# Output projection of a hybrid diffusion layer: seven half-size products in place of eight, with the norm, the stores and the neighbouring sums laid out anew

## The chip, the cores and the metric

The kernel runs on one core of a Trainium2 chip. The metric is the device time of one execution in microseconds (us), the median of several runs. The engines are TensorE (PE; its weight loads are listed as PEld), VectorE (DVE), ScalarE (ACT), GpSimd (POOL) and SyncE (SP), which issues the DMAs. Each works through its own list of instructions in order and waits on semaphores of the others.

## What is computed

One layer over 1024 latent tokens of width 1024. Its part that matters here, with `merged` the gated sum of an attention and a retention branch:

```python
y  = (merged) @ w_out                 # 1024 x 1024 by 1024 x 1024
x1 = x + gate1 * y                    # gated residual
n  = x1 * rsqrt(mean(x1 * x1, -1) + 1e-6)
h2 = n * (g2 * (1 + scale2)) + shift2 # modulated, feeds the gated MLP
u  = h2 @ w_up ; conv ; silu-gate ; @ w_down
out = final_norm(x1 + gate2 * mlp)
```

## The kernel before

**Numbers.** Every fp32 operand is split into a high part and a remainder (`split`, L85: a cast on ScalarE, L86, and a subtraction on VectorE, L87). A product is three matmuls: high by high, high by low, low by high (`mm3`, `open3` at L1372).

**Seven products.** Several matrix products are done by the Strassen-Winograd scheme: both operands are cut into 2 by 2 quarters, sums S1 to S4 of one and T1 to T4 of the other are formed, and seven products of quarters take the place of eight (`Seven`, L1376). That holds before the change for the merge gates, the up projection (from its third unit on; a unit is the product for one pair of column blocks) and the down projection, but not for the output projection.

**Stages around the change**, in the order of the text, which is nearly the order on each engine:

- *Gates* (748 to 924 us): the products of the merge gates. Beside them POOL makes sums of quarters of `w_down` (`down_sums`, L1238, subtraction at L1249): SP loads four tiles `pj` of 128 x 512, POOL makes four subtractions, SP stores the four results to `d_w`, from which the down projection loads them later. Blocks 0 to 4 are made beside retention, blocks 5 to 8 here (at every third step, L1540), blocks 9 and 10 in the next stage.
- *Merge* (924 to 1007 us): for each of 8 channel blocks `db` and both token halves `pret` (L1588) multiplies retention by its projection, VectorE multiplies by the gate, POOL adds the attention part (L1593), and the result is split into `mh`, `ml`. SP loads `w_out`, split into `wo` (L1620 to L1636).
- *Output projection* (1007 to 1100 us): `out_proj` (L1638) goes over 8 blocks of 128 tokens and two column halves, 24 matmuls into a bank `om` each (L121 to L123). VectorE multiplies by `gate1` (L1650) and adds the rows of `x` (L1651); SP stores the rows `x1`; ScalarE squares them and sums (L1654), VectorE and POOL turn that into the norm's factor (L1655, L1656), VectorE scales (L1657, `xn`). `norm_out` (L1660) of the block before transposes `xn` on PE, and ScalarE and VectorE modulate it into `h2` (L1677 to L1680); in the second half VectorE makes the token sums T1 to T4 of each block (L1686 to L1689) and SP stores them to `d_t`.
- *Up projection* (from about 1100 us): two plain units (L1838) whose products need no sums, with the depthwise convolution `conv` (L1754) after each; `comb` (L1780) loads and splits the token sums T1 and T2 in the first, T3 and T4 in the second. Then come the units in seven products, interleaved. The first product with a T operand is the second one of unit 2. Their weight sums are made on POOL (L1383 to L1386).
- *Down projection* (L1858 on): seven products of 11 steps, with the sums of products, the gated residual on POOL (L1946, L1947), the squares on ScalarE (L1897) and the final norm.

Of the kernel before, what the change touches and what calls it, by code (L numbers as in the profile page):

```python
# [16 lines left out]
P = 128  # L17
# [23 lines left out]
def tile_hybrid_layer(ctx, tc: tile.TileContext, io, dbg=None):  # L41
# [18 lines left out]
    d_h = dram.tile([NTB // 2, P, KB, P], F32, name="d_h")  # L60
    d_t = dram.tile([4, NTB // 2, P, KB // 2, P], F32, name="d_t")
# [1176 lines left out]
    def down_sums(pool_, j0, j1, bufs=8):  # L1238
        def load(j, n):
            t = pool_.tile([P, 512], F32, tag="pj", bufs=bufs, name="pj")  # L1240
            sync.dma_start(t, io["w_down"][n % 2, NH * (n // 2) + j])
            return t

        ts, store = [load(j0, n) for n in range(4)], None
        yield
        for j in range(j0, j1):
            nxt = []
            for n, (c, x, y, o) in enumerate(((1, 1, 0, 0), (3, 3, 1, 1), (2, 3, 0, 3), (4, 2, 3, 2))):
                late(pool.tensor_tensor(ts[o], ts[x], ts[y], ALU.subtract))  # L1249
                if store:  # L1250
                    sync.dma_start(*store)
                store = (d_w[j, c - 1], ts[o])
                if j + 1 < j1:
                    nxt.append(load(j + 1, n))
# [121 lines left out]
    class Seven:  # L1376
# [24 lines left out]
        def step(self, n):  # L1401
# [7 lines left out]
            elif n == 1:  # L1409
                self.prod(self.Y, self.s2, "T2", True, False)  # L1410
# [150 lines left out]
    gpool = [sb(f"gates{i}", "right") for i in range(2)]  # L1561

    def gtile(half, dt, name):
        return gpool[half].tile([P, 512], dt, tag="g", bufs=2 * KB + 1, name=name)

    sg = {}

    def merge_load(db, halves=(0, 1)):
        for half in halves:
            sg[db, 0, half] = gtile(half, F32, "sg")  # L1570
            sync.dma_start(sg[db, 0, half], d_pn[db, half])
            sg[db, 1, half] = t = gtile(half, F32, "sg")
# [11 lines left out]
    pjp = sb("out_sums", "right")  # L1584
    out_sums = down_sums(pjp, GATE_SUMS, NH, 7)
    mg = {}

    def pret(db, half):  # L1588
        m = g_ps("pr")
        mm_a(m, wp[db], lambda k: orr[half, k][0], lambda k: orr[half, k][1])  # L1590
        g = sg[db, 1, half]
        vec.tensor_tensor(g, m, g, ALU.mult)
        (vec if db == KB - 1 else pool).tensor_tensor(g, g, sg[db, 0, half], ALU.add)  # L1593
        h_, l_ = gtile(half, F32R, "mh"), gtile(half, F32R, "ml")
        split(h_, l_, g)
        mg[db, half] = (h_, l_)


    merge_load(0, (0,))
# [3 lines left out]
    wp[1] = pret_load(1)  # L1603
    merge_load(1, (0,))
    for half in range(2):
        if half:
            merge_load(0, (1,))
            merge_load(1, (1,))
        for db in range(2):
            pret(db, half)  # L1610
    for db in range(2, KB):
        wp[db] = pret_load(db)
        merge_load(db)
        if db == 2:
            brow(0, gate1)
        for half in range(2):
            pret(db, half)
            next(out_sums, None)
    pjp.release()
    wo = {}  # L1620
    for kb in range(KB):
        t = wop.tile([P, 2, 512], F32R, tag="wo", bufs=KB, name="wo")
        wo[kb, 0] = wload(io["w_out"][0, kb], into=t)
# [5 lines left out]
    h2p = sb("h2", "left")  # L1629
    h2 = [[h2p.tile([P, 2, 512], F32R, tag="h2", bufs=KB, name="h2a") for _ in range(KB)], None]  # L1630
    op = sb("outp", "right")
    po = ps("out_ps", "left")
    pu = [ps("u_ps0", "right")]
    for kb in (6, 7, 0, 1, 2, 3, 4, 5):
        t = (wop if kb >= 6 else op).tile([P, 2, 512], F32R, tag="wx", bufs=2, name="wx") if kb >= 4 else None
        wo[kb, 1] = wload(io["w_out"][1, kb], into=t)  # L1636

    def out_proj(tb):  # L1638
        half, ts = tb // 4, slice((tb % 4) * P, (tb % 4 + 1) * P)
        x1 = op.tile([P, D], F32, tag="x1", bufs=3, name="x1")  # L1640
        xr = op.tile([P, D], F32, tag="xn", bufs=2, name="xn")
        sync.dma_start(x1, io["x"][tb * P : (tb + 1) * P])
        for dh in range(2):
            cs = slice(dh * 512, dh * 512 + 512)
            m = po.tile([P, 512], F32, tag="o", bufs=2, name="om")
            for kb in range(KB):
                wc = wo[kb, dh]
                h_, l_ = mg[kb, half]
                mm3(m, h_[:, ts], l_[:, ts], wc[:, 0], wc[:, 1], kb == 0, kb == KB - 1)
            vec.tensor_tensor(xr[:, cs], m, gate1[:, cs], ALU.mult)  # L1650
            vec.tensor_tensor(x1[:, cs], xr[:, cs], x1[:, cs], ALU.add)  # L1651
        sync.dma_start(d_x1[tb * P : (tb + 1) * P], x1)
        ss = op.tile([P, 2], F32, tag="ss", bufs=2, name="ss")
        act.activation(xr, x1, AF.Square, accum_out=ss[:, 0:1])  # L1654
        vec.tensor_scalar(ss[:, 0:1], ss[:, 0:1], 1.0 / D, EPS, ALU.mult, ALU.add)  # L1655
        pool.tensor_tensor(ss[:, 1:2], ss[:, 0:1], mhalf[:, 0:1], ALU.pow)  # L1656
        vec.tensor_scalar(xr, x1, ss[:, 1:2], None, ALU.mult)  # L1657
        return xr

    def norm_out(tb, xr):  # L1660
        half, ts = tb // 4, slice((tb % 4) * P, (tb % 4 + 1) * P)
        if tb == 4:
            h2[1] = [(gtile(0, F32R, "h2h"), gtile(0, F32R, "h2l")) for _ in range(KB)]
        vr = op.tile([P, KB, P], F32, tag="v", bufs=2, name="v")
        if half:
            vo = op.tile([P, KB, P], F32, tag="vo", bufs=1, name="vo")
            sync.dma_start(vo, d_h[tb - 4])
        for kg in range(2):
            tp = po.tile([P, 4, P], F32, tag="t", bufs=2, name="tp2")
            for k in range(4):  # L1670
                pe.transpose(tp[:, k], xr[:, (kg * 4 + k) * P : (kg * 4 + k + 1) * P], ident)
            for k in range(4):
                kb = kg * 4 + k
                t = h2[half][kb]
                h_, l_ = (t[:, 0, ts], t[:, 1, ts]) if half == 0 else (t[0][:, ts], t[1][:, ts])
                a, sh = a2[:, kb : kb + 1], col[:, 24 + kb : 25 + kb]
                act.activation(h_, tp[:, k], AF.Identity, bias=sh, scale=a)  # L1677
                v = vr[:, kb]
                vec.tensor_scalar(v, tp[:, k], a, sh, ALU.mult, ALU.add)  # L1679
                vec.tensor_tensor(l_, v, h_.bitcast(F32), ALU.subtract)  # L1680
        if half == 0:
            sync.dma_start(d_h[tb], vr)
            return

        (b11, b21), (b12, b22) = [(t[:, : KB // 2], t[:, KB // 2 :]) for t in (vo, vr)]
        vec.tensor_tensor(b11, b12, b11, ALU.subtract)  # L1686
        vec.tensor_tensor(b12, b22, b12, ALU.subtract)
        vec.tensor_tensor(b22, b22, b11, ALU.subtract)
        vec.tensor_tensor(b21, b21, b22, ALU.subtract)  # L1689
        for c, t in enumerate((b11, b22, b12, b21)):  # L1690
            sync.dma_start(d_t[c, tb - 4], t)

    xr = None
    for tb in range(NTB):
        nx = out_proj(tb)
        if tb:
            norm_out(tb - 1, xr)
        xr = nx


    def up(u, wu, half):
        h = h2[half]
        hi, lo = ([t[:, i] for t in h] if half == 0 else [t[i] for t in h] for i in range(2))
        mm_a(u[:, half * 512 : half * 512 + 512], wu, lambda k: hi[k], lambda k: lo[k])

    def up_load(j, br):
        return [wload(io["w_up"][j, br, i]) for i in range(2)]

    def u_tile(n):
        return pu[n // 2 % 2].tile([P, T], F32, tag="u", bufs=2, name="u")  # L1710

    early = []
    for br in range(2):
        early.append((u_tile(br), up_load(0, br)))
        up(*early[br], 0)
    norm_out(NTB - 1, xr)
    po.release()
    pu.append(ps("u_ps1", "left"))
# [12 lines left out]
    A11, A12, A22, S1, S2, S3, S4 = range(7)  # L1731

# [47 lines left out]
    def comb(c):  # L1780
        t = [tpl.tile([P, 4, KH, P], F32R, name=f"T{c}{i}") for i in range(2)]
        for b in range(4):
            raw = ur_load(d_t[c, b])
            split(t[0][:, b], t[1][:, b], raw.rearrange("p (k t) -> p k t", k=KH))
# [4 lines left out]
    class Up(Seven):  # L1789
# [11 lines left out]

        def banks(self):
            t = u_tile(2 * self.n)
            self.X, self.Y = t[:, 0:512], t[:, 512:1024]
            self.Z = u_tile(2 * self.n + 1)[:, 0:512]
            self.u = [tap.tile([P, T], F32, tag="uu", bufs=4, name="uu") for _ in range(2)]

        def moving(self, c):
            if c[0] == "T":
                h_, l_ = combs[c]  # L1810
                return [(h_[:, :, k], l_[:, :, k]) for k in range(KH)]
# [3 lines left out]
        def dst(self, b, half):  # L1815
            return self.u[b][:, half * 512 : half * 512 + 512]
# [4 lines left out]
        def done(self, b, half):  # L1821
            if (b, half) == (0, 1):
                conv(self.j, *self.u)

# [262 lines left out]
```

## Time and profile before

| | |
|---|---|
| time, median of 3 runs | 1764.97 us (1764.35 to 1765.2) |
| profiled execution, first to last instruction (span) | 1759.2 us |
| between this span and the median of the runs | 5.8 us |
| TensorE busy | 1726.0 us, 98% |
| VectorE busy | 1284.2 us, 73% |
| ScalarE busy | 849.2 us, 48% |
| GpSimd busy | 539.3 us, 31% |
| mean granted TensorE clock | 0.996 |

The durations come from one profiled execution; the times from separate runs. The profiled execution's own time is known only as its span. The profile names each group of instructions by its line, engine and tiles (output <- inputs); `idle before` is the time that the engine waited ahead of it, with the releaser. Matmuls are pipelined: one lasts 0.39 us in the records, while the next starts earlier, so their rate is read from starts.

### The profile page before, as it was taken

To read this page: it belongs to the slowest core of one execution; us is meant where nothing else is said; L and a number is where in the kernel's file an instruction comes from. 1 tells how busy PE (TensorE), PEld (TensorE's weight loads), DVE (VectorE), ACT (ScalarE), POOL (GpSimd) and SP (SyncE) were. 2 spreads that over 40 slices of the span, in tenths; PEclk is the share of its full clock that TensorE was granted. 3 is DMA by queue.
4 is the path that set the end of the run, shared out by engine and by line. 5 is a ranking of instruction groups with operands and counts; after the bars stand their busy time and mean duration, and the time that the engine had idled before them with its cause. 6 is when DMAs were issued, how large, how long until landed. Compare 5 with 4: busy or idle time off the path is not lost.

```text
span 1759.2 us, 24801 instructions
## 1 busy us (share of the span) xinstructions
PE 1726.0 (98%) x8405; PEld 1429.3 (81%) x8405; DVE 1284.2 (73%) x2454; ACT 849.2 (48%) x1826; POOL 539.3 (31%) x455
## 2 busy tenths in 40 slices
PE   8999999999999999999999999989999999999997
PEld 4688988888888888778888888778888888788886
DVE  4778887756776766777665557868899889875755
ACT  5666666653443434443444324534444444554444
POOL 1000000003334343555413300165555655211444
PEclk9999999999999999999999999999999999999999
DMA  9143334342231212677557733733322332586754
GB/s 348 61 130 125 95 117 147 117 133 87 73 108 43 72 42 68 203 238 239 200 199 268 246 143 132 254 108 102 108 90 92 118 120 90 170 296 192 239 162 162
DMA packets 139408, 261.10 MB, mean 148 GB/s; under 512 B 15856, under 2 KB 28304, under 8 KB 139280
## 3 DMA queue, kind: packets, MB, share of 16 engines
q1 hardware_dynamic: 139280, 259.51, 44.3%
q8 instruction: 66, 1.08, 0.3%
q14 instruction: 62, 0.51, 0.1%
HBM read 187.34 MB, written 69.48 MB: 146 GB/s over the span
## 4 chain that ended last, share of the span: by engine, by line
PE 43%; issue 6%; DVE 4%; POOL 3%; DMA 1%; ACT 1%; SPq 0%; POOLq 0%; ACTq 0%; DVEq 0%
PE u L1374 30%; PE y L1374 4%; PE pr L112 2%; PE pr L111 2%; PE pr L110 2%; PE om L122 1%; PE om L121 1%; PE om L123 1%; POOL x L1902 1%; DVE wc L87 0%; DVE b L1350 0%; DVE v L1679 0%; POOL pd L1939 0%; DVE hxT L87 0%; POOL x L1947 0%
## 5 line engine op out<-in xcount | busy, mean ns | idle before, releaser
L1374 PE MATMUL u<-T,wc 128*128 128x512 f32 x960 | 227.1, 392 | 5.1 <-ACT pu L1408 5.1
L1374 PEld LDWEIGHTS u<-T,wc 128*128 128x128 f32 x960 | 180.6, 189 | 45.7 <-ACT pu L1408 7.9
L1374 PE MATMUL y<-wc,ahl 128*128 128x512 f32 x924 | 210.6, 389 | 2.7 <-DVE wc L87 1.8
L1374 PEld LDWEIGHTS y<-wc,ahl 128*128 128x128 f32 x924 | 173.3, 188 | 39.7 <-DVE wc L87 2.5
L87 DVE TENSOR_TENSOR wc<-ur,wc 128x512 fp32r<-128x512 f32 x137 | 122.7, 897 | 65.8 <-ACT wc L86 65.8
L86 ACT CAST wc<-ur 128x512 fp32r<-128x512 f32 x137 | 85.0, 621 | 129.7 <-PE y L1374 72.3
L111 PE MATMUL mm<-low,wc 128*128 128x512 f32 (+1 forms) x328 | 124.0, 378 | 0.0
L1374 PE MATMUL u<-h2a,wc 128*128 128x512 f32 x480 | 112.3, 389 | 0.7 <-DVE pu L1417 0.7
L110 PE MATMUL mm<-hx,wc 128*128 128x512 f32 x264 | 107.4, 407 | 0.2 <-ACT wc L589 0.2
L1374 PEld LDWEIGHTS u<-h2a,wc 128*128 128x128 f32 x480 | 90.0, 188 | 19.8 <-DVE pu L1417 1.2
L112 PE MATMUL mm<-hx,wc 128*128 128x512 f32 x264 | 105.2, 399 | 0.0
L86 ACT CAST wc<-s 128x512 fp32r<-128x512 f32 x80 | 49.7, 623 | 93.2 <-PE u L1374 88.3
L123 PE MATMUL mm<-wc,low 128*128 128x512 f32 (+1 forms) x240 | 91.2, 380 | 0.0
L1374 PE MATMUL u<-hxT,wc 128*128 128x512 f32 x384 | 89.6, 389 | 0.0
L1508 POOL TENSOR_TENSOR col<-col,bcol 128x32 f32<-128x32 f32 x1 | 0.3, 253 | 280.7 <-DVE aw L538 280.7
L87 DVE TENSOR_TENSOR wc<-s,wc 128x512 fp32r<-128x512 f32 x80 | 83.5, 1046 | 3.8 <-ACT wc L86 3.4
L1374 PEld LDWEIGHTS u<-hxT,wc 128*128 128x128 f32 x384 | 72.1, 188 | 14.9
L87 DVE TENSOR_TENSOR wc<-raw,wc 128x512 fp32r<-128x512 f32 x92 | 68.0, 746 | 17.7 <-ACT wc L86 17.7
L121 PE MATMUL mm<-wc,hx 128*128 128x512 f32 x192 | 75.2, 392 | 0.6 <-ACT r L1105 0.6
L122 PE MATMUL mm<-wc,hx 128*128 128x512 f32 x192 | 75.2, 392 | 0.0
L1383 POOL TENSOR_TENSOR s<-ur 128x512 f32<-128x512 f32 x20 | 35.7, 1783 | 126.3 <-DVE wc L87 68.7
L86 ACT CAST wc<-raw 128x512 fp32r<-128x512 f32 x92 | 56.8, 621 | 33.0 <-PE pr L112 6.0
(393 smaller groups left out, 4671.3 us busy)
## 6 DMA issues: line engine op xcount, KB each, us to landing
ur<-in_w_up SPq DMA_DIRECT2D x80, 256.0 KB, 2.9
ur<-d_a SPq DMA_DIRECT2D x77, 256.0 KB, 3.1
aw<-in_w_ada SPq DMA_DIRECT2D x32, 512.0 KB, 3.3
pj<-in_w_down SPq DMA_DIRECT2D x44, 256.0 KB, 5.2
d_w<-pj SPq DMA_DIRECT2D x44, 256.0 KB, 2.0
d_a<-sa SPq DMA_DIRECT2D x44, 256.0 KB, 2.0
ur<-d_w SPq DMA_DIRECT2D x44, 256.0 KB, 3.8
d_a<-at SPq DMA_DIRECT2D x33, 256.0 KB, 2.7
```

The costliest lines, as they stand in the source:

```text
L86: act.copy(hi, src)
L87: (lo_eng or vec).tensor_tensor(lo, src, hi.bitcast(F32), ALU.subtract)
L110: pe.matmul(out, wh, xh, start=k == 0, stop=False)
L111: pe.matmul(out, wh, xl, start=False, stop=False)
L112: pe.matmul(out, wl, xh, start=False, stop=k == n - 1)
L121: pe.matmul(out, ah, bh, start=first, stop=False)
L122: pe.matmul(out, ah, bl, start=False, stop=False)
L123: pe.matmul(out, al, bh, start=False, stop=last)
L1374: pe.matmul(out, a, b, start=first and n == 0, stop=last and n == 2, skip_group_check=True)
L1383: pool.tensor_tensor(self.s1, self.a21, self.a22, ALU.add)
L1508: pool.tensor_tensor(col[:, 16:48], col[:, 16:48], bcol[:, 16:48], ALU.add)
L1902: pool.tensor_tensor(z, z, fg[:, gs(dh)], ALU.mult)
```

## The change

The output projection becomes seven products of quarters. Its left operand is the merged activation (channels by tokens), its quarters A11 to A22 being channel half by token half; the right operand is `w_out`.

- `weight_sums` takes jobs of either weight. Beside the gates POOL now makes the four sums of each of the 4 block rows of `w_out` (stored to `d_wo`) and blocks 5 to 10 of `w_down`: 40 subtractions at three of four steps, where there were 16; the merge stage makes none.
- The merge goes through the channel blocks in the order 0, 4, 1, 5, 2, 6, 3, 7. Its results stay unsplit in fp32; after each pair VectorE makes S1 to S4 (`mg_sums`).
- Each product has 4 steps of 12 matmuls (4 banks of 128 tokens). A step splits one weight tile `wr` (6 buffers, ahead on SP) and one left operand into `ahl` (4 buffers).
- Rows of `x1` are finished in halves of 512 columns: gate and residual partly on POOL (`gated`), partly on VectorE (`out_last`). ScalarE squares each half row and then issues its store to `d_x1` from its own queue.
- The norm's two halves of the sum are joined on POOL (`out_last`); the transposes work per channel block over 512 tokens (`turn2`): those of tokens 512 to 1023 in the last product and the first up products, the others between further up products. Token sums are made per channel block on VectorE (`token_sums`).
- In the up projection the products B11 and B21 of units 2 and 3 (`head`, `HEADS = 2`) run between the plain units' products and the first use of T; the T operands are loaded and split after them in the text. The plain units' results are copied out of PSUM by ScalarE before `conv`.

PE issues the same instructions in the same order up to the output projection. The core of the diff:

```diff
-    RET_SUMS, GATE_SUMS = 5, 9
-    ret_sums = down_sums(rt, 0, RET_SUMS)
+    DOWN_JOBS = [("w_down", NH, d_w, j) for j in range(NH)]
+    OUT_JOBS = [("w_out", KB // 2, d_wo, j) for j in range(KB // 2)]
+    RET_SUMS = 5
+    ret_sums = weight_sums(rt, DOWN_JOBS[:RET_SUMS])
...
-    gate_sums = down_sums(gr, RET_SUMS, GATE_SUMS)
+    gate_sums = weight_sums(gr, OUT_JOBS + DOWN_JOBS[RET_SUMS:])
...
-        if n % 3 == 1:
+        if n % 4:
             next(gate_sums, None)
...
+    def out_ops(p, js):
+        tl = []
+        for j in js:
+            ask(p * KH + j + 6)
+            w = wtile()
+            split(w[:, 0], w[:, 1], wq[p * KH + j])
+            a = pair_tile("ahl")
+            split(a[:, 0], a[:, 1], am[ORDER[p][0], j])
+            tl.append((j, a, w))
+        return tl
...
+    def out_square(tb, dh):
+        junk = t_tile("junk")
+        act.activation(junk, z[tb, dh], AF.Square, accum_out=ss[:, tb, dh : dh + 1])
+        act.dma_start(d_x1[tb * P : (tb + 1) * P, cols(dh)], z[tb, dh])
+
+    def out_early(tb, dh):
+        out_square(tb, dh)
+        pool.tensor_scalar(ss[:, tb, 2:3], ss[:, tb, dh : dh + 1], 1.0 / D, EPS, ALU.mult, ALU.add)
+
+    def out_last(tb, dh, p, x):
+        z[tb, dh] = t = t_tile("z")
+        vec.tensor_tensor(t, bank(p % 2, tb % QB), gate1[:, cols(dh)], ALU.mult)
+        vec.tensor_tensor(t, t, x, ALU.add)
+        out_square(tb, dh)
+        s = ss[:, tb]
+        pool.tensor_scalar(s[:, 3:4], s[:, dh : dh + 1], 1.0 / D, s[:, 2:3], ALU.mult, ALU.add)
+        pool.tensor_tensor(s[:, 4:5], s[:, 3:4], mhalf[:, 0:1], ALU.pow)
+        xn[tb, 0], xn[tb, 1] = t_tile("xn"), t_tile("xn")
+        vec.tensor_scalar(xn[tb, 0], z[tb, 0], s[:, 4:5], None, ALU.mult)
+        act.activation(xn[tb, 1], z[tb, 1], AF.Copy, scale=s[:, 4:5])
+
+    def gated(t, dh, x):
+        pool.tensor_tensor(t, t, gate1[:, cols(dh)], ALU.mult)
+        pool.tensor_tensor(t, t, x, ALU.add)
...
+    out_steps(0, True, False)
+    for b in range(QB):
+        p1[b] = t_tile("p1")
+        act.copy(p1[b], bank(0, b))
+
+    xa = four_rows(0, 1)
+    out_steps(1, True, False)
+    for b in range(QB):
+        u2[b] = t_tile("u2")
+        vec.tensor_tensor(u2[b], bank(1, b), p1[b], ALU.add)
+    for b in range(QB):
+        gated(u2[b], 1, xa[b])
+
+    xa = four_rows(0, 0)
+    out_steps(2, False, True)
+    for b in range(QB):
+        z[b, 0] = t_tile("z")
+        vec.tensor_tensor(z[b, 0], bank(0, b), gate1[:, cols(0)], ALU.mult)
+        pool.tensor_tensor(z[b, 0], z[b, 0], xa[b], ALU.add)
+        out_early(b, 0)
+
+    xa, xb = four_rows(QB, 0), four_rows(QB, 1)
+    out_steps(3, False, False)
+    for b in range(QB):
+        u3[b] = t_tile("u3")
+        vec.tensor_tensor(u3[b], bank(1, b), p1[b], ALU.add)
+    for b in range(QB):
+        gated(p1[b], 0, xa[b])
+
+    out_steps(4, True, False)
+    for b in range(QB):
+        z[QB + b, 1] = u3[b]
+        vec.tensor_tensor(u3[b], bank(0, b), u3[b], ALU.add)
+        gated(u3[b], 1, xb[b])
+        out_early(QB + b, 1)
+
+    out_steps(5, False, True, 2)
+    tl = out_ops(5, (2, 3))
+    t7 = out_ops(6, (0, 1))
+    for b in range(QB):
+        out_mm(5, b, tl, False, True)
+        if b == 1:
+            t7 += out_ops(6, (2, 3))
+        out_last(QB + b, 0, 5, p1[b])
+
+    for n in range(2):
+        for b in range(QB):
+            out_mm(6, b, t7[n : n + 1], False, True)
+    for b in range(QB):
+        turn2(1, KORD[b], bank(1, 2 + b % 2))
+        out_mm(6, b, t7[2:], False, True)
+        out_last(b, 1, 6, u2[b])
+    seq = [j + NH * i for j in range(NH) for i in range(2)]
+    wu = [[up_load(seq[1], br) for br in range(2)], [up_load(seq[0], 0), up_load(seq[0], 1, (pair_tile("w"), pair_tile("w")))]]
+    for n, k in enumerate(KORD):
+        if n + QB < KB:
+            turn2(1, KORD[n + QB], bank(1, 2 + n % 2))
+        for br in range(2):
+            up_k(us4[br], wu[0][br], 1, k, n)
+    for n, k in enumerate(KORD):
+        turn2(0, k, bank(0, n % 2))
+        if k >= KH:
+            token_sums(k - KH)
+        for br in range(2):
+            up_k(us4[2 + br], wu[1][br], 1, k, n)
...
+        if n == 0:
+            for i in range(PLAIN, PLAIN + HEADS):
+                units[i].head()
+            for c in (1, 0, 2, 3):
+                combs[f"T{c + 1}"] = comb(c)
     for i, n in interleaved(PLAIN, NF):
-        units[i].step(n)
+        if i >= PLAIN + HEADS or n not in (0, 4):
+            units[i].step(n)
```

`turn2` transposes 4 times 128 x 128 of `xn` into one bank, modulates it on ScalarE (`h2`, high part) and VectorE (`v`, then `h2l` as `v` minus the high part). The order of the products is (A11, B11), (S2, T2), (A12, B21), (S3, T3), (S1, T1), (A22, T4), (S4, B22).

More of the change, by code (lines that the diff above doesn't have):

```diff
@@ L1617, in tile_hybrid_layer @@
             pret(db, half)
[L1618 to L1623, printed above, removed]
+        if db >= KH:
+            mg_sums(db - KH)
     hxpool.release()
@@ L1629, in tile_hybrid_layer @@
     h2p = sb("h2", "left")
+    op = sb("outp", "right")
+    pu = ps("u_ps", "right")
     h2 = [[h2p.tile([P, 2, 512], F32R, tag="h2", bufs=KB, name="h2a") for _ in range(KB)], None]
[L1631 to L1658, printed above, removed]
```

250 lines of the change are left out of this document (140 added, 110 removed).

## The prediction

> **What bounds the kernel now.** I read the page first, for which engine is full and where it is not, then the busy time by stage, then TensorE's waits from the merge on.
>
> ```profile
> PE 1726.0 (98%) x8405; PEld 1429.3 (81%) x8405; DVE 1284.2 (73%) x2454; ACT 849.2 (48%) x1826; POOL 539.3 (31%) x455
> PE   8999999999999999999999999989999999999997
> ```
> ```profile
> 836.00:880.00 44.00, 44.00 (x196) 36.42 (x194) 28.18 (x36) 18.18 (x30) 21.27 (x15) 1.00 0.58 196
> 968.00:1012.00 44.00, 44.00 (x196) 36.45 (x195) 25.76 (x39) 15.87 (x28) 14.96 (x12) 1.00 0.75 247
> 1056.00:1100.00 44.00, 44.00 (x207) 36.51 (x206) 32.44 (x89) 17.76 (x41) 2.19 (x4) 1.00 0.35 135
> 1140.00:1160.00 20.00, 14.85 (x59) 11.87 (x58) 15.89 (x19) 7.93 (x12) 15.09 (x8) 0.91 0.38 119
> ```
> ```profile
> PE u L1374 <- ACT pu L1408: 5.1, 1, 5.1
> PE u L111 <- DVE h2l L1680: 0.6, 2, 0.3
> ```
>
> TensorE is the bound: 98% of the span. After each stretch's limits and length stand PE, PEld, DVE, ACT and POOL with their counts, then clock, DMA share, GB/s. Gate products (836 to 880), merge (968 to 1012) and output projection (1056 to 1100) fill PE: 44.00 of 44 us. The waits list PE's only idle time from 860 to 1230, almost all one gap of 5.1 us. So a removed matmul is worth its full pitch, and every wait that the new order puts on PE costs its full length. The timeline gives pitch and gap:
>
> ```profile
> 1147.63 2.88 PE L1374 MATMUL u<-h2a,wc 128*128 128x512 f32 x12
> 1150.35 1.07 PE L1374 MATMUL u<-T,wc 128*128 128x512 f32 x4
> 1156.57 9.09 PE L1374 MATMUL u<-T,wc 128*128 128x512 f32 x32 [5.15 <-ACT pu L1408]
> 1165.49 2.88 PE L1374 MATMUL u<-h2a,wc 128*128 128x512 f32 x12
> ```
>
> From start to start: twelve matmuls take 1150.35 - 1147.63 = 2.72 us, 0.2267 each.
>
> **What is gained.** Eight output banks by 8 blocks by 2 halves by 3 matmuls were 384; seven products of 4 steps by 4 banks by 3 are 336. 48 fewer by 0.2267: **-10.9 us**.
>
> The gap stood at the first product with T operands (sums of the modulated tokens, stored, loaded, split). The next matmul was due at 1150.35 + 4 x 0.2267 = 1151.26 and came at 1156.57, 5.3 late; the 32 behind it took 1165.49 - 1156.57 = 8.92 instead of 7.25, 1.7 more. The change stores the sums earlier and puts 48 matmuls (10.9 us, products B11 and B21 of two units) ahead of the first use of T: **-7.0 us**. Bounds 0 and -7.0; I take all, because 10.9 us of cover exceeds 5.3.
>
> **What is hidden.** Beside the gates POOL makes 40 subtractions instead of 16, 24 more, with 24 loads and stores each:
>
> ```profile
> L1249 POOL TENSOR_TENSOR pj<-pj 128x512 f32<-128x512 f32 x16 | 26.4, 1655 | 7.5 <-DMA pj<-in_w_down 7.0
> ```
>
> 24 x 1.655 = 40 us on a POOL that is busy 21.27 of 44 over four such stretches: it fits. DVE there has 28.18 of 44; its splits stretch beside POOL (rows below: 0.69 alone, up to 1.78), so 24 x 1.1 = 26 us more over 176 us, 35 of 44. Cost 0 to +3; I take 0. The merge stage loses 16 casts and 16 subtractions of mh/ml, 8 POOL sums and 16 weight splits, and gets 16 DVE subtractions: 0 to +2 at the hand-over of the PSUM banks to product 0; I take 0. The sixteen row stores now issue on ScalarE. The trace has none there; SP's cost 0.33 to 0.38 (row below), 6 us on an engine with 26 of 44 free: 0 by itself, though each sits behind a Square.
>
> **What is lost.** Engines run their lists in order, so I went through the lists of the new out stage as built, with t = 0 at product 0, 48 x 0.2267 = 10.9 us a product, 2.72 a step. The nearest thing in the trace is the last stage, already in seven products, where POOL adds, ScalarE squares and POOL scales in turn:
>
> ```profile
> 1687.28 1.29 POOL L1946 TENSOR_TENSOR x<-x,gate 128x512 f32<-128x512 f32 x1 [39.23 <-DVE x L1945]
> 1689.90 3.45 POOL L1946 TENSOR_TENSOR x<-x,gate 128x512 f32<-128x512 f32 x2
> 1703.28 1.29 POOL L1947 TENSOR_TENSOR x<-x,xr 128x512 f32<-128x512 f32 x1
> 1705.41 0.19 POOL L1901 TENSOR_SCALAR ssf<-ssf 128x1 f32<-128x1 f32 x1 [0.84 <-ACT xr L1897]
> 1705.68 1.30 POOL L1902 TENSOR_TENSOR x<-x,fg 128x512 f32<-128x512 f32 x1
> ```
> ```profile
> 1704.60 0.63 ACT L1897 ACTIVATE xr<-x 128x512 f32<-128x512 f32 x1 [4.89 <-POOL x L1947]
> 1705.14 0.18 ACT L1897 ACTIVATION_READ_ACCUMULATOR xr<-x 128x1 f32 x1
> 1705.23 0.60 ACT L86 CAST wc<-ur 128x512 fp32r<-128x512 f32 x1
> 1705.74 0.62 ACT L86 CAST ahl<-ur 128x512 fp32r<-128x512 f32 x1
> ```
> ```profile
> 1688.91 1.57 DVE L87 TENSOR_TENSOR wc<-ur,wc 128x512 fp32r<-128x512 f32 x1
> 1690.41 1.78 DVE L87 TENSOR_TENSOR ahl<-ur,ahl 128x512 fp32r<-128x512 f32 x1
> ```
>
> A POOL add costs 1.29 alone and 1.73 beside DVE's splits; add, Square, scale and the next add take 1705.68 - 1703.28 = 2.40. While a Square waits for POOL, ScalarE's casts wait behind it (4.89 idle), and operands stop coming. There the operand buffers held 8; here `ahl` has 4.
>
> *A, in product 3.* Product 1's first bank closes at 19.8 and DVE's adds follow its splits, so POOL gets the eight gate operations on `u2` at about 21.2 and ends at 31.5 (1.29 each) to 35.0 (1.73). Then come four rounds for `z`; the fourth Square ends 3 x 2.40 + 1.29 + 0.84 = 9.3 later, at 40.8 to 44.3. Behind those four Squares in ScalarE's list stands the cast of product 3's fourth operand; with the subtraction it is ready at 42.1 to 45.6, and PE asks for it at 32.6 + 3 x 2.72 = 40.8. Loss 1.3 to 4.8: **+3.0**.
>
> *B, at product 6.* By the same count, 3.0 later: POOL starts on `p1` at 45.0 and is through at 55.3 to 58.8; product 4 closes its first bank at 55.4, its sum is there at 56.1, and POOL is through with the gates of `u3` at 66.4 to 72.6; the fourth Square ends at 67.3 to 73.5, the casts of product 6 stand behind it (ready 1.8 later), and PE wants them at 68.3. Loss 0.8 to 7.0: **+4.0**.
>
> *C, the norm of tokens 512 to 1023.* The rows of the last blocks and of the present norm give one round:
>
> ```profile
> 1748.60 0.69 DVE L1971 TENSOR_TENSOR z<-y,gate 128x512 f32<-128x512 f32 x1 [0.64 <-PE y L1374]
> 1748.76 0.33 SPq L1911 DMA_DIRECT2D out_dram<-x  x1
> 1749.18 0.38 SPq L1912 DMA_DIRECT2D out_dram<-z  x1
> 1749.33 0.69 DVE L1972 TENSOR_TENSOR z<-z,pd 128x512 f32<-128x512 f32 x1
> 1750.11 0.64 ACT L1897 ACTIVATE xr<-z 128x512 f32<-128x512 f32 x1 [1.38 <-DVE z L1972]
> 1750.94 0.26 POOL L1906 TENSOR_SCALAR ssf<-ssf 128x1 f32<-128x1 f32 x1 [1.82 <-ACT xr L1897]
> 1751.28 0.55 POOL L1907 TENSOR_TENSOR ssf<-ssf,mhalf 128x1 f32<-128x1 f32 x1
> ```
> ```profile
> L1657 DVE TENSOR_SCALAR xn<-x,ss 128x1024 f32<-128x1024 f32 x8 | 6.0, 754 | 5.4 <-POOL ss L1656 5.4
> ```
>
> Product, add, Square, scale, power: 1748.60 to 1751.83. With the scaling of half a row (half of 0.754) that is 3.7 us. In DVE's new list block 5's product stands behind block 4's scaling, so the four blocks go one after the other. From the middle of B (Squares end at 70.4, product 6 starts at 72.3): five casts, then block 4's Square at 73.0, its `xn` at 75.2, the others at 78.9, 82.6 and 86.3. PE has 24 matmuls of product 6 ahead of the first transposes (77.7), five ahead of block 6's, three ahead of block 7's: late by 1.2, 2.5 and 3.0. **+6.7**; from 3 (chain free to start when product 5's banks close) to 11 (5 us a round, with splits between).
>
> *D, the norm of tokens 0 to 511.* Here DVE's list goes round with `v` and `h2l` of one 128-channel block (0.6 each) inside each round: 3.7 + 1.2 = 4.9 us from one `h2l` to the next. PE needs one for every 6 matmuls and 4 transposes, 1.8 us by the pitch (estimating 0.1 for a transpose). With the last `xn` of C at X, `h2l` come at X + 2.4, 7.3, 12.3, 17.2 and 21.6; PE is ready for the second at X + 5.4, having 16 matmuls of product 6 left. Late by 1.9, 3.2, 3.1, 2.5: **+10.7**; from 0 through 5.7 (round 3.7) to 15 (three splits outside the wait). *E.* After that only the 16 token sums lie on DVE between the `v` and `h2a` of the other half, 2.4 us a block against 1.8 on PE, with two blocks of lead: 0 to +4, **+1**.
>
> Sum: 3.0 + 4.0 + 6.7 + 10.7 + 1 = 25.4 lost, 10.9 + 7.0 = 17.9 gained: +7.5. The profiled span becomes 1759.2 + 7.5 = 1766.7. The profiled execution's time outside its span isn't listed by itself; the median of the runs is 1764.97 - 1759.2 = 5.8 us above the span, and I add that: **1772.5 us**.
>
> The clock. After 5.15 us of idle time the grant fell:
>
> ```profile
> 1154.00:1158.00 4.00, 1.43 (x3) 1.16 (x4) 3.21 (x4) 3.03 (x5) 3.16 (x3) 0.81 0.28 79
> 1158.00:1162.00 4.00, 4.00 (x15) 3.23 (x14) 3.56 (x5) 0.63 (x1) 1.98 (x2) 0.77 0.37 111
> ```
>
> That cost 1.7 us. My pieces are mostly of 3 us or less, so I add nothing; if it went in proportion to idle time, 25.4 / 5.15 x 1.7 = 8.4 more, 1781. The Trainium skill, page "TensorE: Matmul & The Clock Gate", section "HAM oscillation — how this bites in real kernels", says that only an idle gap above about 3.4 us throttles TensorE again. By that rule only B pays: an estimate of 1.7 us, 1774; the row of 5.15 agrees, and none here shows a gap of 3.
>
> **The rivals.**
> 1. *The norm chains are covered* (faster). Up matmuls and product 6 hide C and D, because DVE's product of the next block runs inside the wait for the last. It decides from a round under 1.8 us a block. 1772.5 - 17.4 = 1755. For it: the present norm costs PE 0.6 us in all. Against: today a block has 48 matmuls beside it, here 6. Chance 0.20.
> 2. *Nothing is lost* (faster): 1764.97 - 17.9 = 1747. For it: in the last stage, with the same blocked casts, PE waited 2.7 us from 1540 on:
>
> ```profile
> PE y L1374 <- DVE wc L87: 1.8, 2, 1.4
> PE y L1374 <- ACT wc L86: 0.9, 1, 0.9
> ```
>
>    Against: it has 8 buffers and 11 steps a product. Chance 0.08.
> 3. *The T gap stays* behind later token sums, and the change doesn't do this part: 1779.5. Against: 10.9 us of matmuls are put before it. Chance 0.07.
> 4. *Gates crowd*: POOL's 24 sums slow DVE beyond its splits' lead in the gate stage, 26 us of stretching of which a third reaches PE, +9: 1781. Against: 9 of 44 us of DVE stay free. Chance 0.05.
>
> **How the numbers follow.** My forecast, waits above gains, has 0.60; of it 0.12 lies at or below no change, where its low ends meet (A 1.3, B 0.8, C 3, D 5.7, E 0 make 10.8: 1758). About 0.2% (3.5 us) is what measurement can tell from no change. Faster: 0.28 from rivals 1 and 2, 0.03 from low ends; same 0.09; slower 0.60. Range 1752 to 1786: its low end leaves out rival 2; its high end takes in rivals 3 and 4 and most of the upper bounds (41.8 lost would be 1789). Forecast's own range: 1762 to 1784.
>
> **What would show it.** PE waiting for ScalarE's `ahl` casts in the fourth step of product 3 and at product 6; PE waiting for DVE's `xn` before the transposes, then for `h2l` in steps of about 4.9 us; no gap at the first T product; gate stage at 44.00 of 44. I am wrong if PE is full through products 3 to 6 and the first up unit, or if `h2l` come every 2 us.

## The result, and the profile after

The changed kernel took 1830.17 us (median of 4 runs, 1827.11 to 1833.13) against 1765.09 for the kernel before (1764.35 to 1765.74): 1.037 times as long, 95% interval 1.0353 to 1.0388. Forecast were 1772.5 us, with a range of 1752 to 1786. The profiled span is 1831.4 us, 72.2 more than before; it is the longest of the four executions (1825.3 to 1831.4). The page of the changed kernel:

```profile
PE 1747.5 (95%) x8357; PEld 1436.5 (78%) x8357; DVE 1328.4 (73%) x2394; ACT 860.2 (47%) x1842; POOL 612.8 (33%) x515
...
PE   8999999999999999999899888889999999999997
```

TensorE has 48 matmuls fewer and is busy 21.5 us longer (1726.0 before). Idle it is 1831.4 - 1747.5 = 83.9 us instead of 33.2. So the 72.2 us are 50.7 more of idle time, 10.9 less of matmuls at full rate, and a remainder of 32.4. The remainder is the lower clock: a mean granted clock of 0.979 over 1831.4 us is worth 38.5 us at full rate, 0.996 over 1759.2 us was worth 7.0, which makes 31.4 more. The digits below 9 lie in two places, beside the gates and from the output projection on. The same by stage, cut at the first TensorE instruction of each in the profiled executions (the last stage from the last up matmul on; in brackets TensorE's idle time, without the 8 us behind its last matmul):

| us | before | after | more |
|---|---|---|---|
| up to the gates | 768.4 | 770.6 | 2.2 |
| gates | 152.4 (0.0) | 182.6 (18.2) | 30.2 |
| merge | 87.0 (0.0) | 89.8 (1.5) | 2.8 |
| first output product to last up product | 531.5 (6.5) | 563.3 (35.0) | 31.8 |
| down projection | 219.9 (2.7) | 225.1 (3.8) | 5.2 |

The busy time by stage, in the columns of the prediction's table (span, PE, PEld, DVE, ACT, POOL, clock, DMA share, GB/s):

```profile
836.00:880.00 44.00, 39.64 (x165) 31.72 (x164) 32.07 (x32) 13.89 (x24) 29.45 (x19) 0.96 0.72 248
880.00:924.00 44.00, 36.15 (x144) 28.96 (x143) 25.60 (x32) 15.89 (x28) 25.99 (x18) 0.92 0.74 259
...
1056.00:1100.00 44.00, 38.78 (x166) 31.63 (x165) 27.65 (x33) 19.54 (x39) 18.93 (x16) 0.95 0.52 178
```

Beside the gates no engine is full: VectorE is busy 32 and 26 of 44 us, POOL 29 and 26. Something makes them wait in turn. TensorE's waits name VectorE and ScalarE as the last link:

```profile
PE u L1377 <- DVE pu L1424: 10.8, 5, 4.2
PE u L1377 <- DVE wc L87: 10.6, 5, 5.3
PE u L1377 <- ACT ahl L86: 10.1, 2, 5.2
PE u L1377 <- DVE pu L1418: 6.3, 2, 3.7
PE u L1735 <- DVE xn L1721: 5.8, 4, 2.0
```

The two lines with `pu` are the gate stage (but for 1.1 us at the T gap), `ahl` is the forecast's A and B, `xn` its C and D, and the 5.3 us in `wc` are the hand-over to product 0. What those engines waited for shows in SP's own list. Its longest rows of waits from 775 to 925 us, first of the kernel before, then of the changed one:

```profile
SPq L1251 <- POOL pj L1249: 33.0, 11, 5.9
SPq L1482 <- DVE c L1481: 30.3, 15, 5.5
```
```profile
SPq L1252 <- POOL pj L1250: 56.4, 23, 8.9
SPq L1489 <- DVE c L1488: 12.3, 7, 5.0
```

SP stands 56.4 us before stores of weight sums that POOL hasn't made, 23.4 more than before. Its waits as such aren't the loss: over all rows of this stretch they add up to 87.4 us before, where TensorE never idled beside the gates, and to 77.2 after. What counts is which loads stand behind them. One such stop in the changed kernel's timeline, SP's list first, then POOL's:

```profile
863.63 0.32 SPq L1252 DMA_DIRECT2D d_w<-pj  x1
864.36 0.33 SPq L1242 DMA_DIRECT2D pj<-in_w_down  x1
873.88 0.32 SPq L1252 DMA_DIRECT2D d_w<-pj  x1
874.25 0.42 SPq L1242 DMA_DIRECT2D pj<-in_w_down  x1
```
```profile
865.71 1.29 POOL L1386 TENSOR_TENSOR wr<-wr 128x512 f32<-128x512 f32 x1 [7.27 <-DMA wr<-in_w_gate]
...
870.52 1.63 POOL L1389 TENSOR_TENSOR wr<-wr 128x512 f32<-128x512 f32 x1
872.11 8.53 POOL L1250 TENSOR_TENSOR pj<-pj 128x512 f32<-128x512 f32 x5
```

From 864.7 to 873.9 SP issues nothing: its next store waits for a `pj` subtraction, which stands on POOL behind the four sums of a gate's weights `wr`; those had waited 7.27 us for loads that SP issued only from 858.45 to 862.05, after a stop of the same kind from 840.9 to 850.0. Each waits for the other once a round, and loads for ScalarE and VectorE stand in the same queue.

### The profile page after: what moved, and what is told of

It reads as the page before. It is cut to its first block, busy times and chain, and to the rows that moved or that the text cites. A ratio compares the mean times of both kernels' runs of the same rounds, so it can differ in the third digit from the quotient of the medians.

```text
span 1831.4 us, 24897 instructions
## 1 busy us (share of the span) xinstructions
PE 1747.5 (95%) x8357; PEld 1436.5 (78%) x8357; DVE 1328.4 (73%) x2394; ACT 860.2 (47%) x1842; POOL 612.8 (33%) x515
## 4 chain that ended last, share of the span: by engine, by line
PE 34%; issue 8%; DVE 7%; POOL 5%; DMA 4%; ACT 1%; SPq 1%; POOLq 0%; DVEq 0%; ACTq 0%
PE u L1377 24%; PE y L1377 4%; DVE wc L87 2%; DMA o<-d_oret 1%; PE pr L111 1%; PE pr L112 1%; PE pr L110 1%; DVE c L1488 1%; POOL x L2025 1%; DMA pj<-in_w_down 1%; PE u L123 1%; PE u L122 1%; DMA d_orr<-c 0%; PE u L121 0%; DVE b L1353 0%
## 5 line engine op out<-in xcount | busy, mean ns | idle before, releaser
L87 DVE TENSOR_TENSOR wc<-wr,wc 128x512 fp32r<-128x512 f32 x84 | 91.4, 1104 | 32.9 <-ACT wc L86 32.8
L1377 PE MATMUL u<-hxT,wc 128*128 128x512 f32 x384 | 98.5, 414 | 16.0 <-DVE pu L1424 9.7
L1377 PEld LDWEIGHTS u<-hxT,wc 128*128 128x128 f32 x384 | 76.7, 201 | 35.2 <-ACT wc L86 11.7
L1377 PE MATMUL u<-wc,ahl 128*128 128x512 f32 x336 | 87.5, 423 | 15.5 <-ACT ahl L86 10.1
L1377 PEld LDWEIGHTS u<-wc,ahl 128*128 128x128 f32 x336 | 68.5, 207 | 32.2 <-ACT ahl L86 11.0
L1250 POOL TENSOR_TENSOR pj<-pj 128x512 f32<-128x512 f32 x60 | 87.1, 1457 | 13.0 <-DMA pj<-in_w_out 9.8
L87 DVE TENSOR_TENSOR wc<-s,wc 128x512 fp32r<-128x512 f32 x80 | 87.2, 1092 | 3.9 <-ACT wc L86 3.5
```

The source lines that it names most:

```text
L87: (lo_eng or vec).tensor_tensor(lo, src, hi.bitcast(F32), ALU.subtract)
L1377: pe.matmul(out, a, b, start=first and n == 0, stop=last and n == 2, skip_group_check=True)
```

## The experiments

The theory after the two traces: beside the gates SP's queue and POOL hold each other up; from the output projection on the forecast's A to D are there, and the hand-over and the T gap beside them. The rivals for the gates are too many bytes and VectorE slowed by POOL. Each kernel was run and profiled once; the stage lengths, cut as in the table, carry the verdicts. Where an edit doesn't touch a stage, the stretch from the first output to the last up product repeats within 1.1 us (562.2 to 563.3); the gate stage spreads over 6.3 (179.2 to 185.5), so a difference of 3 us there says nothing.

**The gate stage without subtractions, and without transfers.**

```diff
# g_nosub, beside the gates
-                late(pool.tensor_tensor(ts[o], ts[x], ts[y], ALU.subtract))
# g_nodma, beside the gates
-                if store:
-                    sync.dma_start(*store)
-                if i + 1 < len(jobs):
-                    nxt.append(load(jobs[i + 1], n))
```

> Beside the gates the 40 POOL subtractions are left out; each tile is stored as it was loaded, so the same 40 loads and 40 stores remain (the sums, and what is made of them, are then not those of the reference). Theory 1, SP's queue blocked by stores that wait for POOL: the gate products take 182 us in the changed kernel and 152 before; they go back to 152 to 156. Theory 2, too many bytes on the DMA queues: they stay within 175 to 182. Theory 3, POOL's port use stretches VectorE: back to 152 to 156 as under theory 1.

> Beside the gates the 40 POOL subtractions stay, on four tiles loaded once; the 36 further loads and all 40 stores are left out, and where their results would be read, quarters of the weights are read in their place (not the reference's values). Theory 1, SP blocked by stores: gates back to 152 to 157. Theory 2, bytes: 152 to 157 too. Theory 3, POOL's port use stretches VectorE: stays at 170 to 182. With the run without subtractions: both short means the coupling through SP.

Measured: 155.8 us without subtractions (1802.8 in all) and 153.9 without transfers (1797.0), from 182.6. Neither the bytes alone nor POOL's work alone costs more than 3.4 us; together they cost 30. So the loss takes both at once, which fits the coupling through SP's queue and goes against theories 2 and 3 as sole causes. By which path the two act on each other these runs don't show.

**The same sums, stored one later.**

```diff
-                if store:
-                    sync.dma_start(*store)
-                store = (d[j, c - 1], ts[o])
+                store.append((d[j, c - 1], ts[o]))
+                if len(store) > 2:
+                    sync.dma_start(*store.pop(0))
```

> The same sums, loads and stores beside the gates, but each store is issued one sum later on SP, when POOL has most likely made it. Theory 1: the gate stage falls from 182 to 155 to 168, as SP seldom waits. Theories 2 and 3: 178 to 182, since nothing else changes.

Measured: 170.0 us (11.6 idle), 1819.5 in all: outside the 155 to 168 of theory 1, and further outside the 178 to 182 of the others. 12.6 us go by the place of a store in SP's list alone. That the rest stays because SP still waits is likely but not shown; its waits from 775 to 925 us:

```profile
SPq L1253 <- POOL pj L1250: 44.3, 20, 7.7
```

**The stores on POOL's queue.**

```diff
-                    sync.dma_start(*store)
+                    pool.dma_start(*store)
```

> As the changed kernel, but beside the gates the 40 stores of the weight sums issue from POOL's own queue, behind the subtraction that makes them; SP only loads. Theory 1, SP's queue blocked: the gate stage (182 us, 20 idle) falls to 153 to 162, the most of all edits that keep sums and bytes, since no load on SP then stands behind POOL. Rival, the sheer load of POOL and the DMA queues together: it stays above 168, where one sum of delay had left it at 170.

Measured: 173.9 us (14.4 idle), 1818.5 in all. The expected 153 to 162 is missed, and the rival's "above 168" is met. SP's waits in this kernel, from 775 to 940 us, show where they went:

```profile
SPq L1242 <- DMA d_wo<-pj: 21.2, 12, 5.6
SPq L1489 <- DVE c L1488: 20.6, 10, 4.4
SPq L1242 <- POOL pj L1250: 17.5, 5, 6.3
SPq L1242 <- DMA d_w<-pj: 14.8, 9, 3.4
```

Now the loads of `pj` (L1242) stand on SP until one of eight buffers is free, that is until POOL and the store are through. So SP is blocked still, by another instruction. But the edit brings a cost of its own: a store occupies POOL for 0.56 us in this trace, 22 us for the 40, and its median time to landing is 4.3 and 4.7 us, where it was 3.4 and 3.6 from SP. This run doesn't decide between the blocked queue and the rival, the sheer load of POOL and the DMA queues together.

**That part alone in the kernel before.** Gate stage as in the changed kernel (40 sums at three of four steps), none in the merge stage, the output projection as before; the sums of `w_out` are stored and not used.

> The kernel before with one part of the change alone: 40 weight sums beside the gates at three of four steps, none in the merge stage; the sums of w_out are stored and not used. Theory, SP's queue blocked by their stores: its gate stage grows from 152 to 175 to 185 and the time by 22 to 35 us, to 1787 to 1800. Rival, the gate stage suffers only together with the new output stage: under 5 us more.

Measured: gates 181.8 us (21.3 idle), output to last up product 533.7, 1794.9 in all (the kernel before took 1758.4 beside it). The placement of the sums costs 29.4 us in the gate stage by itself, without the new output stage. The time rises by 36.5, a little more than the 22 to 35 expected (the 1794.9 lie within its 1787 to 1800); the profiled span is 33.8 above that of the kernel before, 4.4 of them outside the gates.

**The sums dealt out anew.**

```diff
-    RET_SUMS = 5
-    ret_sums = weight_sums(rt, DOWN_JOBS[:RET_SUMS])
+    RET_SUMS = 6
+    ret_sums = weight_sums(rt, OUT_JOBS + DOWN_JOBS[:RET_SUMS])   # two at each place
...
-        if n % 4:
+        if n % 3 == 1:
```

> The changed kernel with the sums dealt out anew: 40 beside retention (those of w_out first), 20 beside the gates at one of three steps, as densely as before the change. Theory: the gate stage goes from 182 back to 152 to 155 and retention loses at most 3 us, so 25 to 31 us less than the changed kernel, about 1800. Rival, the sums cost their time wherever they stand: retention grows by 10 us or more.

Measured: gates 156.8 us, but 784.1 up to the gates instead of 770.6; 1818.7 in all. The rival holds for half: 25.8 us are gained beside the gates and 13.5 lost again ahead of them. In retention TensorE now waits for VectorE in steps that show no wait in the kernel before:

```profile
PE tpo L1200 <- DVE A L1174: 8.0, 10, 1.5
```

**A and B: the Squares behind the casts.**

```diff
     for b in range(QB):
         pool.tensor_tensor(z[b, 0], z[b, 0], xa[b], ALU.add)
-        out_early(b, 0)
     out_steps(3, False, False)
+    for b in range(QB):
+        out_early(b, 0)        # likewise the four behind product 4:
+    t7 = out_ops(6, (0, 1))    # behind these
```

> Only the place of the Squares and stores of rows on ScalarE moves: those behind product 2 to behind product 3's casts, those behind product 4 to behind the casts of the first two steps of product 6. Theory 1, casts blocked behind Squares that wait for POOL (A and B): TensorE's two waits for ahl of 5.2 and 4.9 us go, and with them 2 to 3 us of low clock each, 12 to 16 us in all. Rival: VectorE and POOL are late anyhow, the wait moves to another releaser, under 4 us saved.

Measured: output to last up product 556.6, 6.7 us less (1822.7 in all). In TensorE's waits the 10.1 for `ahl` become

```profile
PE u L1377 <- DVE ahl L87: 3.5, 5, 1.4
...
PE u L1377 <- ACT ahl L86: 2.3, 1, 2.3
```

A is gone. At B 2.3 us remain for a cast, now two steps later, in the third step of product 6, where it stands behind the moved Squares. The 3.5 us for VectorE's splits are new and lie in products 4 to 6, so a part of the wait moved on to VectorE, as the rival had it. In all it is half of the expected 12 to 16.

**C and D: two phases.** Product, add and Square of a block are put ahead of power and scaling of the block before (`out_last` cut in two).

```diff
         out_last(QB + b, 0, 5, p1[b])
+        if b:
+            out_norm(QB + b - 1, 0)
```

> Only the order of the norm's steps moves: a block's product, add and Square come ahead of the scaling of the block before it, so that VectorE works while a Square and power are under way. Theory, the serial round of 3.7 and 4.9 us (C and D): of TensorE's 9.9 us of idle time at the transposes and h2l, 6 or more go, 6 to 10 us in all with the clock. Rival, the blocked Squares set the chain's start and its rounds matter little: under 3 us.

Measured: 553.7, 9.6 us less (1823.6 in all). That is within the expected 6 to 10. In TensorE's waits only this is left of the 5.8 for `xn`:

```profile
PE u L1737 <- DVE xn L1723: 1.4, 2, 1.2
PE u L1737 <- ACT xn L1724: 1.3, 2, 1.1
```

**The first product's operands.** Its splits are written ahead of the last merge evacuation, the last `mg_sums` behind the product.

```diff
+    tl0 = out_ops(0, range(KH))
+    last()                       # the evacuation of the last merge bank
...
+    mg_sums(KH - 1)              # behind product 0
```

> VectorE's splits of the first product's left operands now stand ahead of the last merge evacuation, and the last four activation sums behind the product's operands. Theory: the 5.3 us that TensorE waits at the first product for VectorE's split weights fall to 1 to 2, and 2 us of low clock behind them go: 5 to 7 us. Rival, the weight tiles land late (their loads issue 2 to 7 us ahead): 2 us or less.

Measured: 554.7, 8.6 us less (1821.6 in all), more than the expected 5 to 7. TensorE's timeline of this kernel:

```profile
1041.77 3.47 PE L1377 MATMUL u<-wc,ahl 128*128 128x512 f32 x14 [1.16 <-DVE wc L87]
```

1.16 us in the place of 5.29.

**The T gap: loads first, no heads, convolution later.**

```diff
# t_raw: weights and sums of unit 2 first, T through three tiles of its own
+            units[PLAIN].load()
-            split(t[0][:, k], t[1][:, k], ur_load(d_t[c, k]))
+            split(t[0][:, k], t[1][:, k], rawload(d_t[c, k]))
# heads0
-    PLAIN, HEADS = 2, 2
+    PLAIN, HEADS = 2, 0
# t_conv: held until step 2 of unit 2, pinned in VectorE's list
-        conv(seq[n], *uu)
```

> The loads and POOL sums of the weights of unit 2 stand ahead of the loads of the T operands, which go through three tiles of their own, no longer through the same twelve. Theory: POOL's sum waits 53 us for weights that queue behind 16 loads of T, so the T gap (9 us idle, some 6 of clock) goes or falls under 4: 8 to 14 us. Rival, T itself is late (as the prediction held of the kernel before): the gap stays or grows, as T now loads three tiles at a time.

> The changed kernel without the products B11 and B21 of units 2 and 3 ahead of the first use of T (they come in their usual places; the matmuls are as many). Theory, T is ready at a fixed time and the 48 matmuls do cover it: without them the gap grows by 8 to 11 us and the stretch from the first output product to the last up product from 563 to 571 to 576. Rival, VectorE is full from the convolution on and its work, not T, sets the pace: 561 to 567.

> The changed kernel with the convolution of the second plain unit held back behind the splits for the second T product. Theory, its four VectorE operations of 1.3 to 2.3 us in front of that split make TensorE's wait of 4.2 us: it goes, with some 2 us of low clock, 557 to 559 in the place of 563. Rival, VectorE has too much to do there in whatever order: the wait moves to the next split or sum, 562 to 564.

Measured, from the first output to the last up product: t_raw 566.6 (1836.0 in all), heads0 573.0 (1841.8), t_conv 558.8 (1825.2). Loading the weights first makes it 3.3 us worse, so the expected gain of 8 to 14 did not come. It doesn't clear the weights' loads, though, because the edit changed two things. POOL's first sum is made at 1209.6 instead of 1221.5, but T now loads through three tiles, ScalarE waits 11.5 us for these loads, and the last split of T ends at 1244.3 instead of 1221.5: one late operand was exchanged for another. Without the heads the stretch grows by 9.7 us, and the idle time of the T gap from 9.7 to 16.1. So the 48 matmuls do cover, and the operands' chain, not TensorE, sets the time of the first T product: it comes 180.7 us behind the first output product without the heads and 181.8 with them.

That T itself is what is ready at a fixed time is not borne out. In the changed kernel, T's last split, POOL's first sum of unit 2, the cast of such a sum on ScalarE, and TensorE's first T product:

```profile
1220.85 0.69 DVE L87 TENSOR_TENSOR T<-ur,T 128x512 fp32r<-128x512 f32 x1 [0.48 <-ACT T L86]
1221.46 1.29 POOL L1386 TENSOR_TENSOR s<-ur 128x512 f32<-128x512 f32 x1 [53.03 <-DMA ur<-in_w_up]
1224.14 0.62 ACT L86 CAST wc<-s 128x512 fp32r<-128x512 f32 x1 [3.32 <-POOL s L1387]
1224.81 0.74 PE L1377 MATMUL u<-T,wc 128*128 128x512 f32 x2 [1.44 <-ACT wc L86]
```

All of T is split by 1221.5, and the four tiles of T2, which this product takes, by 1213.8. TensorE waits for the product's weights, a POOL sum of tiles whose loads SP issues from 1214.4 on, behind the sixteen loads of T.

Holding back the convolution saves 4.5 us, as expected and more than the rival allowed; a wait of 3.36 us for a split remains.

**The stores' queue.**

```diff
-        act.dma_start(d_x1[tb * P : (tb + 1) * P, cols(dh)], z[tb, dh])
+        sync.dma_start(d_x1[tb * P : (tb + 1) * P, cols(dh)], z[tb, dh])
```

> The changed kernel with the sixteen half-row stores on SP's queue in place of ScalarE's. Theory: the place of the issue costs ScalarE 0.4 us each behind Squares that wait anyway; out to last up product 563 plus or minus 2. Rival, the issue on ScalarE delays the casts behind it: 4 us or more less.

Measured: 562.5, 0.8 us less (1830.6 in all), within the repeat. The queue of these stores does not matter here.

**All four together** (moved, sq_late, c_two, p0_first).

> Sums dealt out anew, Squares and stores behind the casts, the first product's operands ahead of the last evacuation, the norm's steps in two phases: all four together. If the four losses are independent, the parts found singly add up (30 + 7 + 9 + 10): about 1774, with 537 us from the first output product to the last up product (563 in the changed kernel, 531 before). If they share a bottleneck on VectorE, the sum falls short: 545 or more there, 1782 or more.

Measured: 542.5 from the first output to the last up product, 1800.3 in all. The stretch lies between the two expectations (537, and 545 or more); the time is above both. That stretch gains 20.8 of the 24.9 us that the parts gained singly; it is still 11.0 longer than before, with 23.5 us of idle time. The sums in retention and beside the gates still cost another 22. No version run here comes below the kernel before.

## Why the prediction was wrong, step by step

**The step that failed: "Beside the gates POOL makes 40 subtractions instead of 16 ... it fits. Cost 0 to +3; I take 0."** It cost 30.2 us. The working asked whether POOL and VectorE had time left, and they had. It did not ask what stands behind each new store in SP's list: 24 more stores that wait for POOL, ahead of loads that POOL waits for. SP's waits at the same stores in the kernel before, 33.0 us, had been there to read. Shown are the place (29.4 us with this part alone) and that it takes the subtractions and the transfers together (each alone at most 3.4 us). The path through SP's list is shown for 12.6 us, which go by one sum of delay; for the rest it is argued. Rival 4 was at the right place with another mechanism (VectorE slowed by POOL) and a third of the price.

**The clock: "I add nothing."** It is the second failure. In the gate stage 30.2 us are 18.2 of idle time and 12 of matmuls at a lower clock; over the span it is 32.4 beside 50.7. In proportion to the idle time (1.7 per 5.15, the alternative that I worked out and set aside) 50.7 would give 16.7, half of what came. The step rested on "none here shows a gap of 3", and that was misread. The kernel before has one ahead of the gates, and the granted clock fell behind it:

```profile
719.84 1.97 PE L1366 MATMUL tpn<-ident,onr 128*128 128x128 f32 x8 [3.27 <-DVE ona L1369]
```
```profile
719.00:723.00 4.00, 3.17 (x12) 2.87 (x13) 4.00 (x8) 3.95 (x8) 4.00 (x4) 0.57 0.69 251
```

**The hand-over to product 0: "0 to +2 ... I take 0."** It was 5.3 us, and then 2.6 because the 84 matmuls behind the wait took 21.85 us instead of 19.2; the experiment gave 8.6 back. TensorE's and VectorE's rows:

```profile
1043.02 1.07 PE L1377 MATMUL u<-wc,ahl 128*128 128x512 f32 x4
1049.38 21.85 PE L1377 MATMUL u<-wc,ahl 128*128 128x512 f32 x84 [5.29 <-DVE wc L87]
```
```profile
1043.22 0.69 DVE L1599 TENSOR_TENSOR sg<-pr,sg 128x512 f32<-128x512 f32 x1 [4.02 <-PE pr L112]
...
1048.64 2.50 DVE L87 TENSOR_TENSOR wc<-wr,wc 128x512 fp32r<-128x512 f32 x4
```

VectorE sat 4.0 us idle at the evacuation of the last merge product, with the weights' subtractions behind it and behind four activation sums. The list was at hand; I had priced the stage by its totals.

**The T gap: -7.0.** It is 9.7 us of idle time instead of 5.15. The cover of 10.9 us was nearly right (9.7 without it); the step that failed is what it was to cover. I took the gap for a wait for T. In the kernel before, VectorE's last splits of T and a later cast on ScalarE:

```profile
1140.10 3.69 DVE L87 TENSOR_TENSOR T<-ur,T 128x512 fp32r<-128x512 f32 x6
1152.85 0.62 ACT L86 CAST wc<-ur 128x512 fp32r<-128x512 f32 x1 [4.21 <-DMA ur<-in_w_up]
```

T was split by 1143.8, 6.6 us ahead of the first T product at 1150.35. The gap's row names a copy on ScalarE (L1408), and ScalarE's list had just stood 4.2 us before a cast whose weights had not landed. So already there the row pointed at the weights and at ScalarE's list; no run changes this in the kernel before, so it is read from the trace alone. In the changed kernel the first part of the gap is weights again, as shown at the experiments. VectorE's rows at the second part, and TensorE's behind them:

```profile
1230.64 2.31 DVE L1874 SCALAR_TENSOR_TENSOR at<-uu,cw,at 128x1023 f32<-128x1023 f32 x1
...
1235.08 1.27 DVE L1875 SCALAR_TENSOR_TENSOR at<-uu,cw,at 128x1023 f32<-128x1023 f32 x1
1236.27 0.68 DVE L87 TENSOR_TENSOR wc<-s,wc 128x512 fp32r<-128x512 f32 x1
```
```profile
1237.00 9.65 PE L1377 MATMUL u<-T,wc 128*128 128x512 f32 x30 [4.18 <-DVE wc L87]
```

The convolution's four operations, two of them stretched from 1.27 to 2.3 beside POOL, stand ahead of one split of weights; holding the convolution back gave 4.5 us. How much the weights' late loads cost by themselves stays open.

**Right: the places of A to D.** They were right, and so were the rounds. A: the fourth step of product 3, 5.2 us for +3.0 (1.3 to 4.8); here the timeline of POOL and then ScalarE in product 3:

```profile
1089.94 1.30 POOL L1778 TENSOR_TENSOR z<-z,xr 128x512 f32<-128x512 f32 x1
...
1092.35 1.26 POOL L1778 TENSOR_TENSOR z<-z,xr 128x512 f32<-128x512 f32 x1
```
```profile
1096.02 0.63 ACT L1705 ACTIVATE junk<-z 128x512 f32<-128x512 f32 x1 [1.65 <-POOL z L1778]
...
1096.65 1.12 ACT L86 CAST ahl<-s 128x512 fp32r<-128x512 f32 x2
```

A round of 1092.35 - 1089.94 = 2.41 us (2.40 forecast), and the cast behind the fourth Square. B: 4.9 for +4.0. In C the scalings follow every 3.8 us (forecast 3.7, though its rows add up to 3.6):

```profile
1134.26 0.49 DVE L1721 TENSOR_SCALAR xn<-z,ss 128x512 f32<-128x512 f32 x1 [0.80 <-POOL ss L1719]
...
1138.08 0.49 DVE L1721 TENSOR_SCALAR xn<-z,ss 128x512 f32<-128x512 f32 x1 [0.80 <-POOL ss L1719]
```

In D the `h2l` come 5.0, 5.6, 4.8 and 4.3 us apart (forecast 4.9, and 4.4 for the last). In idle time C cost 3.2 us for +6.7, D 6.7 for +10.7, E nothing for +1. TensorE was slower by then (granted clock 0.77 from 1139 to 1154 us) and so needed the blocks later; that this accounts for the difference was not tried. A to E sum to 20.0 us of idle time for 25.4. The matmuls' -10.9 holds by their count; no run shows it by itself.

From the first output to the last up product +7.5 were forecast and 31.8 came: 28.5 of idle time (20.0 of A to E, 5.3 of the hand-over and 9.7 of the T gap, less the 6.5 of before), 10.9 less of matmuls, and a remainder of 14.2 at a lower clock (0.97 over the stretch, 1.00 before). Of the 5.2 us in the down projection 1.1 are idle time, and some 3 come from a granted clock of 0.50 from 1806 to 1812 us, behind a wait of 2.0 us for a cast; the other kernels of these experiments show 221.4 to 224.8 there. Of the 2.2 us ahead of the gates 1.2 are idle time; the rest stays unexplained.

## What to carry to other kernels

When work goes to an engine with time left, list what each of its DMAs stands in front of on the issuing queue: here stores that waited for a busy producer held up the loads behind them, the producer waited for some of these loads, and VectorE, ScalarE and POOL all looked partly idle. Read the queue's own waits in the profile of before, not for their sum but for what stands behind them. Where a gap names a releaser, follow that engine's list back before naming the operand that was late. And where TensorE is full, price each new wait with the low clock that follows it, here two thirds as much again as the wait.

## What the runs showed of the hardware

A short gap was enough for the clock. Of the changed kernel's gate stage, TensorE's timeline and the busy time in stretches of 4 us:

```profile
821.49 0.50 PE L1377 MATMUL u<-hx,wc 128*128 128x512 f32 x1 [1.38 <-ACT wc L86]
...
822.78 1.22 PE L1377 MATMUL u<-hx,wc 128*128 128x512 f32 x2 [0.56 <-DVE wc L87]
...
833.65 5.72 PE L1377 MATMUL u<-hxT,wc 128*128 128x512 f32 x24 [1.36 <-DVE pu L1424]
...
856.36 7.32 PE L1377 MATMUL u<-hxT,wc 128*128 128x512 f32 x24 [2.88 <-DVE pu L1424]
```
```profile
822.00:826.00 4.00, 3.44 (x9) 2.54 (x9) 4.00 (x3) 2.04 (x4) 3.92 (x4) 0.58 0.53 198
...
856.00:860.00 4.00, 3.64 (x10) 2.88 (x11) 3.00 (x5) 2.07 (x4) 2.36 (x2) 0.60 1.05 373
```

After 1.36 us of idle time 24 matmuls took 5.72 us, after 2.88 us 7.32: 1.6 more, at a granted clock of 0.60. Yet two waits of 1.38 and 0.56 us close together were followed by 0.58, and in the kernel before a wait of 1.36 us that ended at 86.35 by 0.72 over 86 to 92 us. So the length of a single gap doesn't decide whether the clock falls; what does isn't settled by these runs. The rule that the prediction took from the Trainium skill ("TensorE: Matmul & The Clock Gate", "HAM oscillation — how this bites in real kernels": only gaps above about 3.4 us throttle) does not hold for these gaps; the measurement decides.
